# A two-layer hybrid trunk on one core: stationary-weight products as three matmuls of 256 columns in one PSUM bank instead of 512 and 256 in two

## The chip, the cores and the metric

The kernel runs on one core of one Trainium2 chip, with one launch. The metric is the device time of the program in microseconds. TensorE (PE in the profile, with its weight loads under PEld) multiplies, VectorE (DVE) and ScalarE (ACT) work element by element, GpSimd (POOL) does little here, and SyncE (SP) issues nearly all transfers.

## The reference

256 tokens of width 2048 in float32 go through two layers. Cut to what matters:

```python
for layer in range(2):
    if layer == 0:
        x = x + hybrid_mixer(rms_norm(x, hyb_norm), w_in, ..., w_out)   # SSD heads and stick-breaking attention
    else:
        x = x + multiscale_pool(rms_norm(x, pool_norm), pool_w, pool_b, pool_scale)
    u = relu(rms_norm(x, mlp_norm[layer]) @ w_up[layer])                # 2048 -> 8192
    x = x + (u * u) @ w_down[layer]                                     # 8192 -> 2048
```

`hybrid_mixer` projects with `w_in` (2048 columns wide input, about 11,300 columns of output: z, x, B, C, dt, q, k, v), runs a causal convolution, a chunked state-space scan and an attention with stick-breaking weights, and projects with `w_out`.

## The kernel before, in words

**The weight stream.** All products with weights form one list of units (`plan`, lines 47 to 90). A unit is a block of output columns; a step of it is the part of its weights that one DMA brings. The main loop (lines 789 to 827) goes through units and steps in this order; `feed` loads steps ahead (line 161, six ahead) and splits them ahead (lines 182 and 183, three ahead).

**Three products for one.** Each float32 weight is split into a high part (ScalarE, line 182, tile `hi`) and the rest (VectorE, line 183, tile `lo`), and so are the activations: a token tile is `[128, 2, 4, 256]`, that is high and low, four k-tiles, 256 tokens, and the high and low parts of one k-tile stand 4 x 256 float32 = 4 KB apart in a partition. A product is then high x high, high x low and low x high, accumulated in PSUM.

**Two kinds of units.** In most units the tokens are stationary: line 820 loads 128 tokens of a k-tile as weights and streams up to 512 columns of `hi` or `lo`; for each of the two halves of the tokens (m = 0, 1) there are three such matmuls into one bank. The last 512 columns of the last "down" product are cut into two units of 256 columns. In the units marked `turned` the weights are stationary, so that the result has the channels on the partitions: the unit c1, the eight units x of the input projection and the 64 units "up" of the two MLPs, 73 in all, each with 16 k-tiles and 256 output columns in two halves f of 128. Here line 812 loads the 128 columns of `hi` and streams 512 columns, the high part and the low part of the tokens side by side, into one bank for f; and line 814 loads the 128 columns of `lo` and streams the 256 columns of the high part into the first half of the same bank. Each f has a bank of its own. At the end the two halves of each bank must be added.

**The end of a unit.** `finish` reads the accumulators. For turned units `add_halves` (lines 269 to 272) copies the second halves of both banks to SBUF on ScalarE (line 271) and adds the first halves on VectorE (line 272). Then `turned` (line 325) multiplies by the norm's scale per token, and for "up" units line 746 takes the maximum with 0 and multiplies by the same scale.

**Order of the work.** Each engine does its instructions in the order in which the program issues them. Work that is not a product with weights (norms, transposes, convolution, scan, attention) is written as generators in two queues, `lane` and `lane2`; after each step of the stream `tick` advances them by a piece, so their small matmuls stand between those of the stream. The accumulators are two tiles of two banks (`ps_main`, line 791), used in turn, so a unit can begin while the one before is read out.

Of the kernel before, what the change touches and what calls it, by code (L numbers as in the profile page):

```python
# [13 lines left out]
ALU = mybir.AluOpType  # L14
# [3 lines left out]
T = 256  # L18
# [6 lines left out]
NB = DFF // FB  # L25
WINS = (2, 4, 8, 16)

# columns of the input projection: z | x | B | C | dt | q | k | v
CZ, CX, CB, CC = 0, 2048, 4096, 4608
CQ, CK, CV = 5152, 7200, 9248  # L30

# per-partition parameters (channel = tile * 128 + partition)
P_HYB, P_MLP, P_POOL, P_CW, P_CB, P_ON, P_QN, P_KN = 0, 16, 48, 64, 160, 184, 200, 201
NPRM = 202

# constant matrices
K_ID, K_U, K_SL, K_ONE, K_LT = 0, 128, 256, 384, 512
NCST = 640

# where in the weight stream (unit, k-tile) the quarters of x for the first norm are loaded  # L40
X_EARLY = ((0, 14), (1, 2), (1, 6), (1, 10))
AHEAD_LOAD = 6
WARM = 2
# [1 line left out]


def plan():
    """The products with weights in their order. A unit is a block of output columns; a step is
    the part of its weights that one DMA brings: [128, k-tiles, columns]."""
    units = []  # L50

    def unit(w, r0, nk, c0, n, kind, arg, src, k0=0, turned=False):
        units.append(dict(w=w, r0=r0, nk=nk, c0=c0, n=n, kind=kind, arg=arg, src=src, k0=k0,
                          turned=turned))

    unit("w_in", 0, KT, CB, 512, "b", None, "h")
    unit("w_in", 0, KT, CC + 256, 288, "c2", None, "h")
    unit("w_in", 0, KT, CC, 256, "c1", None, "h", turned=True)
    for g in range(4):
        for h in range(2):  # L60
            unit("w_in", 0, KT, CX + 512 * g + 256 * h, 256, "x", (g, h), "h", turned=True)
        unit("w_in", 0, KT, CZ + 512 * g, 512, "z", g, "h")
    for j in range(4):
        unit("w_in", 0, KT, CK + 512 * j, 512, "k", j, "h")
        unit("w_in", 0, KT, CQ + 512 * j, 512, "q", j, "h")
        unit("w_in", 0, KT, CV + 512 * j, 512, "v", j, "h")
    for c in range(4):
        unit("w_out", 0, 2 * KT, 512 * c, 512, "out", c, "merged")
    for layer in range(2):
        if layer == 1:  # L70
            for g in range(4):
                unit("pool_w", 512 * g, 4, 0, 512, "pool", g, "pool", 4 * g)
        for b in range(NB):
            for i in range(8):
                unit("w_up", D * layer, KT, b * FB + 256 * i, 256, "up", (layer, b, i),
                     f"mlp{layer}", turned=True)
            for c in range(4):
                n = 256 if (layer, b, c) == (1, NB - 1, 3) else 512
                for c0 in range(512 * c, 512 * c + 512, n):
                    unit("w_down", DFF * layer + b * FB, KT, c0, n, "down", (layer, b, c), "u")  # L80

    steps, off = [], 0
    for u, d in enumerate(units):
        ks = list(range(0, d["nk"], 4 if d["turned"] else 2))
        if u == 0:
            ks = [0, 1, 2, 3] + ks[2:]
        for k, e in zip(ks, ks[1:] + [d["nk"]]):
            steps.append((u, k, e - k, off))
            off += (e - k) * P * d["n"]
    return units, steps  # L90
# [3 lines left out]
def tile_trunk(ctx: ExitStack, tc: tile.TileContext, x_in, xt_in, w_all, prm_in,  # L94
# [27 lines left out]
    def v3(ap, a, b):  # L122
        return ap.rearrange("p (a b) -> p a b", a=a, b=b)

    # ------------------------------------------------------------ constants
    x_sb = []
    cst = new("cst", [P, NCST])
    prm = new("prm", [P, NPRM])
# [7 lines left out]
        return prm[:, i : i + 1]  # L136

    def load_x(q):
        """half of the tokens' rows, half of the columns at a time"""
        m, c = q // 2, slice(D // 2 * (q % 2), D // 2 * (q % 2) + D // 2)  # L140
        if q == 0:
            x_sb[:] = [slot(12 + m, (P, D), F32) for m in range(MT)]
        nc.sync.dma_start(x_sb[m][:, c], x_in[m * P : m * P + P, c])

    # ------------------------------------------------------------ the weight stream
    hT, merged = {}, {}
    u_blk, pT, hM = {}, {}, [{}, {}]
    sources = {"h": hT, "merged": merged, "pool": pT, "mlp0": hM[0], "mlp1": hM[1], "u": u_blk}
# [42 lines left out]
            split(done["split"])  # L191
            done["split"] += 1

    # ------------------------------------------------------------ work beside the weight stream
    lane, lane2 = deque(), deque()
    flags = set()

# [14 lines left out]
            assert lane or lane2  # L212
            tick()

    # ------------------------------------------------------------ norms
    def power(dst, src, mean):
        """dst = (src * mean + eps) ** -0.5"""
        n = src.shape[-1]
        t = new("pw", [P, 8], bufs=2)[:, :n]
        dve.tensor_scalar(t, src, mean, EPS, ALU.mult, ALU.add)  # L220
        pool.tensor_tensor(dst, t, mhalf[:, :n], ALU.pow)  # L221

    def put_hi_lo(dst, c, ps, gain=None):
        """dst[:, 0/1, c] = the high and low parts of ps (times a per-partition gain)"""
        if gain is None:
            act.activation(dst[:, 0, c], ps, AF.Copy)  # L226
            dve.tensor_tensor(dst[:, 1, c], ps, dst[:, 0, c].bitcast(F32), ALU.subtract)  # L227
        else:
            act.activation(dst[:, 0, c], ps, AF.Copy, scale=gain)  # L229
            dve.scalar_tensor_tensor(dst[:, 1, c], ps, gain, dst[:, 0, c].bitcast(F32),  # L230
                                     ALU.mult, ALU.subtract)

    def to_ring(src, tiles, kt0, dst, gain):
        """src[m]: [128 tokens, 512]; four k-tiles of 256 tokens into dst and tiles[kt0...]"""
        for h in range(2):
            b = bank()
            bv = v3(b, 2, T)
# [15 lines left out]
    rs = {}  # L253

    def spread(name):
        """rs[name, "row"][p, t] = rs[name] of token t, for all p"""
        r = rs[name]
        dg = v3(t4(2 * P), MT, P)
        for m in range(MT):
            dve.tensor_scalar(dg[:, m], ident, r[:, m : m + 1], None, ALU.mult)  # L260
        yield
        b = bank()
        for m in range(MT):
            pe.matmul(b[:, m * P : (m + 1) * P], ones, dg[:, m], start=True, stop=True)
        o = new("rrow", [P, T], bufs=2)
        dve.tensor_copy(o, b[:, :T])
        rs[name, "row"] = o

    def add_halves(dst, ps):
        """dst = the sum of the two halves of each bank"""  # L270
        act.activation(dst, ps[:, :, T:], AF.Copy)  # L271
        dve.tensor_tensor(dst, ps[:, :, :T], dst, ALU.add)  # L272

    def row2(name):
        return rs[name, "row"][:, None, :].to_broadcast([P, 2, T])
# [19 lines left out]
        if c == 3 and name != "pool":  # L295
            yield from spread(name)

    # ------------------------------------------------------------ SSD
    ssd = {}

    def evac(ps, n, r):
# [3 lines left out]
        return e  # L305

    def turn(e, n):
        """e: [tokens, n * 128 channels] -> [channel, n, 3 + 256 tokens]"""
        yield
        yield  # L310
        xT = v3(t4(n * 259), n, 259)
# [9 lines left out]

    def turned(ps):
        xT = v3(t4(2 * 259), 2, 259)
        add_halves(xT[:, :, 3:], ps)
        dve.tensor_tensor(xT[:, :, 3:], xT[:, :, 3:], row2("hyb"), ALU.mult)
        return xT

    def conv(xT, ct0, n, dst):
        """xT: [channel, n, 3 + 256 tokens] -> dst [channel, n, 256 tokens] = silu(conv + b)"""
        dve.memset(xT[:, :, 0:3], 0.0)  # L330
        for c in range(n):
            w = P_CW + 4 * (ct0 + c)
# [7 lines left out]
                yield  # L340

    def gen_dt(pre):
        """pre: [128, 64] dt before softplus, (chunk, head)"""
        e, t, q, da = (ssd["tmp"][:, 1792 + 64 * i : 1856 + 64 * i] for i in range(4))
        # log1p(e) = 2 artanh(e / (2 + e)), e = exp(-|pre|) in (0, 1]
        act.activation(e, pre, AF.Abs)
        act.activation(e, e, AF.Exp, scale=-1.0)
        dve.tensor_scalar(t, e, 2.0, None, ALU.add)
# [153 lines left out]
        dst = slot(8 + g)  # L502
        yield from to_ring(lambda m: y[:, m], merged, 4 * g, dst, P_ON)

    # ------------------------------------------------------------ stick-breaking attention
    at = {}

    def gen_qk(kind, j, e):
# [113 lines left out]
                merged[16 + 4 * j + 2 * i + h] = (dst, 2 * i + h)  # L622
            yield

    # ------------------------------------------------------------ MLP and pooling
    def gen_u(i, ea, eb, base):
        yield
        act.activation(eb, ea, AF.Square)  # L628
# [36 lines left out]
    def finish(u, ps):  # L665
# [73 lines left out]
        elif kind == "up":  # L739
# [2 lines left out]
            need(lambda: (name, "row") in rs)  # L742
            e = ev()
            ea, eb = v3(e[:, 0], 2, T), v3(e[:, 1], 2, T)
            add_halves(ea, ps)
            dve.scalar_tensor_tensor(ea, ea, 0.0, row2(name), ALU.max, ALU.mult)  # L746
            lane.append(gen_u(i, ea, eb, ((4, 8), (0, 4))[layer][b % 2]))

    # ------------------------------------------------------------ the stream
    act.dma_start(prm, prm_in)  # L750
    act.preload_act_table_set("silu_and_others")
    mhalf = new("mhalf", [P, 8])
    pool.memset(mhalf, -0.5)
    # keeps the tensor engine's clock up until the first weights are there
    wt = new("ev", [P, MT, 512], bufs=3)
    dve.memset(wt[:, 0], 0.0)
    wb = bank()
# [3 lines left out]
    hx, late = [], []  # L761

    def startup():
        """the first norm's scale and small constants"""
        ss = new("ss", [P, MT, 4], bufs=2)
        for q in range(4):
            m, h = q // 2, q % 2
# [21 lines left out]
    for u, d in enumerate(units):  # L789
# [5 lines left out]
        while i < len(steps) and steps[i][0] == u:  # L795
# [10 lines left out]
            for kk in range(n2):  # L806
                t, c = src[k0 + k + kk]
                first, last = k + kk == 0, k + kk == nk - 1
                if d["turned"]:
                    for f in range(2):  # L810
                        fs = slice(f * P, f * P + P)
                        pe.matmul(ps[:, f].rearrange("p (h t) -> p h t", h=2), hi[:, kk, fs],  # L812
                                  t[:, :, c], start=first, stop=False)
                        pe.matmul(ps[:, f, :T], lo[:, kk, fs], t[:, 0, c], start=False, stop=last)  # L814
                    continue
                parts = [(m, h) for m in range(MT) for h in range(3)]
                if u == 0:
# [74 lines left out]
```

## Time and profile before

| what | value |
|---|---|
| median of three runs | 2215.83 us (2215.49 to 2216.3) |
| span of the profiled execution | 2214.3 us |
| granted TensorE clock | 1.000 |
| TensorE busy, instructions | 2207.0 us, 11045 (and as many weight loads) |
| VectorE busy | 1325.4 us |
| ScalarE busy | 1113.0 us |
| GpSimd busy | 21.7 us |
| read from HBM | 412.57 MB, 187 GB/s |

The profile is of one execution; what lies around its span is not in it, and the median of the runs is 1.5 us above the span. A row of a group gives line, engine, operation, output and inputs, shape, count, then busy time in us and mean duration of one in ns, then the engine's idle time just before these instructions and who ended it. Matmuls are pipelined: the next begins while the one before still drains, so their durations add up to more than the time they take.

### The profile page before, as it was taken

How to read it: one execution, taken by the hardware profiler on the slowest of the kernel's cores; microseconds unless marked ns; L12 is line 12 of the kernel's file. 1: busy time of each engine (PE TensorE's matmuls, PEld its weight loads, DVE VectorE, ACT ScalarE, POOL GpSimd, SP SyncE). 2: the span in 40 equal slices, each digit the busy share in tenths (PEclk: the TensorE clock that was granted, in tenths of full speed). 3: DMA queues.
4: the chain of work that ended last, by engine and by line, in shares of the span. 5: the costliest groups of instructions: out<-in, count | busy, mean ns of one | idle time of the engine just before them, and what ended most of it. 6: DMA issues, size and time to landing. Idle time of an engine off the chain costs nothing.

```text
span 2214.3 us, 28392 instructions
## 1 busy us (share of the span) xinstructions
PE 2207.0 (100%) x11045; PEld 1854.0 (84%) x11045; DVE 1325.4 (60%) x1554; ACT 1113.0 (50%) x1325; POOL 21.7 (1%) x21
## 2 busy tenths in 40 slices
PE   9999999999999999999999999999999999999999
PEld 7888888888888888888888888888888888888888
DVE  6988756655645565555555466577555645655654
ACT  7665456665544454354344345456534534544543
POOL 0000000000000000000000000000000000000000
PEclk9999999999999999999999999999999999999999
DMA  8654555555665566556566666555666656565564
GB/s 300 213 196 162 163 184 167 163 179 170 202 187 184 181 186 186 189 186 189 187 189 190 204 219 190 181 171 163 190 196 187 188 189 190 187 193 191 190 195 148
DMA packets 118630, 416.56 MB, mean 188 GB/s; under 512 B 13344, under 2 KB 16096, under 8 KB 118240
## 3 DMA queue, kind: packets, MB, share of 16 engines
q1 hardware_dynamic: 117632, 413.60, 59.0%
q8 instruction: 86, 1.41, 0.3%
q10 hardware_dynamic: 864, 1.15, 0.2%
q14 instruction: 48, 0.39, 0.1%
HBM read 412.57 MB, written 2.13 MB: 187 GB/s over the span
## 4 chain that ended last, share of the span: by engine, by line
PE 99%; DMA 0%; DVE 0%; ACT 0%; issue 0%; SPq 0%; DVEq 0%; ACTq 0%
PE acc L820 58%; PE acc L812 25%; PE acc L814 13%; PE bg L469 1%; PE bg L241 1%; DMA raw<-w_all 0%; PE bg L526 0%; PE bg L616 0%; PE bg L561 0%; PE bg L437 0%; PE bg L557 0%; PE bg L618 0%; PE bg L474 0%; PE bg L480 0%; DVE lo L183 0%; PE bg L577 0%
## 5 line engine op out<-in xcount | busy, mean ns | idle before, releaser
L183 DVE TENSOR_TENSOR lo<-raw,hi 128x1024 fp32r<-128x1024 f32 (+2 forms) x774 | 931.4, 1205 | 777.5 <-ACT hi L182 762.9
L182 ACT ACTIVATE hi<-raw 128x1024 fp32r<-128x1024 f32 (+2 forms) x774 | 808.5, 1045 | 1033.8 <-PE acc L820 642.7
L820 PE MATMUL acc<-hi,st 128*128 128x512 f32 (+2 forms) x3840 | 1175.2, 389 | 1.4 <-ACT hi L182 1.4
L820 PEld LDWEIGHTS acc<-hi,st 128*128 128x128 f32 x3840 | 709.9, 188 | 153.4 <-ACT hi L182 3.5
L812 PE MATMUL acc<-st,hi 128*128 128x512 f32 x2336 | 826.1, 398 | 0.0
L820 PE MATMUL acc<-lo,st 128*128 128x512 f32 (+2 forms) x1920 | 740.7, 387 | 0.1
L814 PE MATMUL acc<-st,lo 128*128 128x256 f32 x2336 | 654.8, 280 | 0.0
L812 PEld LDWEIGHTS acc<-st,hi 128*128 128x128 f32 x2336 | 438.3, 188 | 106.1 <-issue 1.4
L814 PEld LDWEIGHTS acc<-st,lo 128*128 128x128 f32 x2336 | 440.5, 189 | 2.0 <-issue 1.2
L820 PEld LDWEIGHTS acc<-lo,st 128*128 128x128 f32 x1920 | 360.4, 188 | 78.1 <-DVE lo L183 0.5
L706 DVE TENSOR_TENSOR st<-st,acc 128x512 f32<-128x512 f32 (+1 forms) x74 | 46.5, 669 | 29.1 <-PE acc L820 29.1
L746 DVE SCALAR_TENSOR_TENSOR ev<-ev,rrow 128x512 f32<-128x512 f32 x64 | 44.3, 692 | 2.2
L227 DVE TENSOR_TENSOR st<-ev,st 128x512 fp32r<-128x512 f32 x64 | 44.3, 692 | 0.2
L272 DVE TENSOR_TENSOR ev<-acc,ev 128x512 f32<-128x512 f32 x64 | 43.7, 683 | 0.0
L226 ACT ACTIVATE st<-ev 128x512 fp32r<-128x512 f32 x64 | 40.6, 634 | 2.0
L229 ACT ACTIVATE st<-bg,prm 128x256 fp32r<-128x256 f32 x64 | 28.4, 468 | 24.9 <-DVE st L230 22.8
L628 ACT ACTIVATE ev<-ev 128x512 f32<-128x512 f32 x64 | 39.5, 617 | 0.0
L271 ACT ACTIVATE ev<-acc 128x512 f32<-128x512 f32 x64 | 37.2, 582 | 0.0
L230 DVE SCALAR_TENSOR_TENSOR st<-bg,prm,st 128x256 fp32r<-128x256 f32 x64 | 29.4, 478 | 6.0 <-ACT st L229 6.0
L336 DVE SCALAR_TENSOR_TENSOR t<-t,prm,t 128x256 f32<-128x256 f32 x48 | 19.6, 476 | 0.0
L221 POOL TENSOR_TENSOR qrs<-pw,mhalf 128x8 f32<-128x8 f32 x8 | 15.6, 1952 | 246.4 <-DVE pw L220 246.4
L516 DVE TENSOR_TENSOR ev<-ev,qrs 128x1024 f32<-128x1024 f32 x8 | 9.8, 1225 | 13.5 <-POOL qrs L221 13.5
(155 smaller groups left out, 595.7 us busy)
## 6 DMA issues: line engine op xcount, KB each, us to landing
raw<-w_all SPq DMA_DIRECT2D x746, 512.0 KB, 3.5
raw<-w_all SPq DMA_DIRECT2D x20, 256.0 KB, 3.1
st<-x_in SPq DMA_DIRECT2D x8, 512.0 KB, 5.3
st<-scr SPq DMA_DIRECT2D x8, 512.0 KB, 5.8
raw<-w_all SPq DMA_DIRECT2D x8, 288.0 KB, 4.5
st<-prow_in SPq DMA_DIRECT2D x2, 1024.0 KB, 5.3
st<-xt_in SPq DMA_DIRECT2D x6, 256.0 KB, 6.3
st<-pmat_in SPq DMA_DIRECT2D x1, 768.0 KB, 5.1
```

What stands on the lines that cost most here:

```text
L182: act.activation(hi, raw, AF.Copy)
L183: dve.tensor_tensor(lo, raw, hi.bitcast(F32), ALU.subtract)
L226: act.activation(dst[:, 0, c], ps, AF.Copy)
L227: dve.tensor_tensor(dst[:, 1, c], ps, dst[:, 0, c].bitcast(F32), ALU.subtract)
L271: act.activation(dst, ps[:, :, T:], AF.Copy)
L272: dve.tensor_tensor(dst, ps[:, :, :T], dst, ALU.add)
L628: act.activation(eb, ea, AF.Square)
L706: dve.tensor_tensor(x_sb[m][:, cs], x_sb[m][:, cs], ps[:, m, : d["n"]], ALU.add)
L746: dve.scalar_tensor_tensor(ea, ea, 0.0, row2(name), ALU.max, ALU.mult)
L812: pe.matmul(ps[:, f].rearrange("p (h t) -> p h t", h=2), hi[:, kk, fs], t[:, :, c], start=first, stop=False)
L814: pe.matmul(ps[:, f, :T], lo[:, kk, fs], t[:, 0, c], start=False, stop=last)
L820: pe.matmul(ps[:, m, :n], t[:, h % 2, c, m * P : (m + 1) * P], (hi, hi, lo)[h][:, kk], start=first and h == 0, stop=last and h == 2)
```

## The change

For turned units, the matmul of 512 columns is replaced by two of 256, both into the same columns of PSUM, and the matmul with `lo` goes there too; both halves f share one bank, the first in columns 0 to 255, the second in 256 to 511. So there are three matmuls of 256 columns for each half and k-tile, each with its own weight load (the first two load the same `hi` columns). Only the very first matmul of a unit has the start flag. `add_halves` is gone: the finishing VectorE instruction reads the bank. The rest of the diff removes comments and docstrings.

```diff
-    def add_halves(dst, ps):
-        """dst = the sum of the two halves of each bank"""
-        act.activation(dst, ps[:, :, T:], AF.Copy)
-        dve.tensor_tensor(dst, ps[:, :, :T], dst, ALU.add)
...
     def turned(ps):
         xT = v3(t4(2 * 259), 2, 259)
-        add_halves(xT[:, :, 3:], ps)
-        dve.tensor_tensor(xT[:, :, 3:], xT[:, :, 3:], row2("hyb"), ALU.mult)
+        dve.tensor_tensor(xT[:, :, 3:], v3(ps[:, 0], 2, T), row2("hyb"), ALU.mult)
         return xT
...
             ea, eb = v3(e[:, 0], 2, T), v3(e[:, 1], 2, T)
-            add_halves(ea, ps)
-            dve.scalar_tensor_tensor(ea, ea, 0.0, row2(name), ALU.max, ALU.mult)
+            dve.scalar_tensor_tensor(ea, v3(ps[:, 0], 2, T), 0.0, row2(name), ALU.max, ALU.mult)
...
                 if d["turned"]:
                     for f in range(2):
                         fs = slice(f * P, f * P + P)
-                        pe.matmul(ps[:, f].rearrange("p (h t) -> p h t", h=2), hi[:, kk, fs],
-                                  t[:, :, c], start=first, stop=False)
-                        pe.matmul(ps[:, f, :T], lo[:, kk, fs], t[:, 0, c], start=False, stop=last)
+                        for h in range(3):
+
+                            pe.matmul(ps[:, 0, f * T : f * T + T], (hi, hi, lo)[h][:, kk, fs],
+                                      t[:, h % 2, c], start=first and h == 0 and f == 0,
+                                      stop=last and h == 2, skip_group_check=True)
                     continue
```

## The prediction

> **What bounds the kernel now.** I began with the page: span, busy engines, and the chain of work that ended last.
>
> ```profile
> span 2214.3 us, 28392 instructions
> PE 2207.0 (100%) x11045; PEld 1854.0 (84%) x11045; DVE 1325.4 (60%) x1554; ACT 1113.0 (50%) x1325; POOL 21.7 (1%) x21
> ...
> q8 instruction: 86, 1.41, 0.3%
> ...
> PE 99%; DMA 0%; DVE 0%; ACT 0%; issue 0%; SPq 0%; DVEq 0%; ACTq 0%
> ...
> L820 PE MATMUL acc<-hi,st 128*128 128x512 f32 (+2 forms) x3840 | 1175.2, 389 | 1.4 <-ACT hi L182 1.4
> ...
> L812 PE MATMUL acc<-st,hi 128*128 128x512 f32 x2336 | 826.1, 398 | 0.0
> ...
> L814 PE MATMUL acc<-st,lo 128*128 128x256 f32 x2336 | 654.8, 280 | 0.0
> L812 PEld LDWEIGHTS acc<-st,hi 128*128 128x128 f32 x2336 | 438.3, 188 | 106.1 <-issue 1.4
> ...
> L746 DVE SCALAR_TENSOR_TENSOR ev<-ev,rrow 128x512 f32<-128x512 f32 x64 | 44.3, 692 | 2.2
> ...
> L272 DVE TENSOR_TENSOR ev<-acc,ev 128x512 f32<-128x512 f32 x64 | 43.7, 683 | 0.0
> ...
> L271 ACT ACTIVATE ev<-acc 128x512 f32<-128x512 f32 x64 | 37.2, 582 | 0.0
> ```
>
> TensorE holds 99% of the chain, and its lines show hardly any idle time before them (1.4, 0.0 and 0.0 us). VectorE and ScalarE are busy 60% and 50% of the time and hold 0% of the chain. So the end is set by the rate at which TensorE takes matmuls, one after another, and by nothing else over any length. The mean durations (398 and 280 ns) are of no use as prices, because matmuls overlap. What counts is the distance from one start to the next. For that I read the chain in order of time, whose long pieces are unbroken runs of one line, and then the timeline of TensorE. In the chain, columns are start, length, line and count:
>
> ```profile
> by line: PE acc L820 58.2%; PE acc L812 24.6%; PE acc L814 12.5%; PE bg L469 0.6%; PE bg L241 0.6%; DMA raw<-w_all 0.4%; PE bg L526 0.3%; PE bg L616 0.3%; PE bg L561 0.3%; PE bg L437 0.2%; PE bg L557 0.2%; PE bg L618 0.2%; PE bg L474 0.2%;
> ...
> 834.33 89.57 PE acc L820 x384
> 1014.35 88.53 PE acc L820 x384
> ...
> 1588.09 87.08 PE acc L820 x384
> 1764.81 89.58 PE acc L820 x384
> 1944.03 87.08 PE acc L820 x384
> 2120.75 89.76 PE acc L820 x480
> ```
>
> Between two runs of L820 lies one block of eight "up" units with stationary weights: 8 units x 16 k-tiles x 2 column halves = 256 pairs of one matmul of 512 columns (L812) and one of 256 (L814). In layer 0 such a block lasts from 834.33 + 89.57 = 923.90 to 1014.35, which is 90.45 us or 353.3 ns a pair. In layer 1 it lasts from 1588.09 + 87.08 = 1675.17 to 1764.81, 89.64 us or 350.2 ns a pair; the next lies between 1854.39 and 1944.03, again 89.64. These are the prices of before, all small stalls included.
>
> **The price of three times 256.** The kernel already contains a stretch of the new kind: its last 512 columns of output are done as two units of 256 columns (192 matmuls of L820, each with its own weight load, three in a row into the same columns of one bank). The timeline of TensorE, at the start and at the end of that stretch:
>
> ```profile
> 2187.77 0.40 PE L820 MATMUL acc<-hi,st 128*128 128x256 f32 x2
> 2188.01 0.29 PE L820 MATMUL acc<-lo,st 128*128 128x256 f32 x1
> 2188.13 0.40 PE L820 MATMUL acc<-hi,st 128*128 128x256 f32 x2
> 2188.37 0.28 PE L820 MATMUL acc<-lo,st 128*128 128x256 f32 x1
> 2188.49 0.39 PE L820 MATMUL acc<-hi,st 128*128 128x256 f32 x2
> ...
> 2210.22 0.27 PE L820 MATMUL acc<-lo,st 128*128 128x256 f32 x1
> ```
>
> From the first start to the start of the 192nd are 2210.22 - 2187.77 = 22.45 us over 191 steps: 117.5 ns each, so 352.6 ns for three. That is the same as the 350.2 and 353.3 ns of the pairs. In the pairs themselves the single 256 (L814) shows the same step, here in a layer-1 block:
>
> ```profile
> 1690.65 0.28 PE L814 MATMUL acc<-st,lo 128*128 128x256 f32 x1
> 1690.77 0.39 PE L812 MATMUL acc<-st,hi 128*128 128x512 f32 x1
> 1691.00 0.28 PE L814 MATMUL acc<-st,lo 128*128 128x256 f32 x1
> 1691.11 0.39 PE L812 MATMUL acc<-st,hi 128*128 128x512 f32 x1
> 1691.34 0.28 PE L814 MATMUL acc<-st,lo 128*128 128x256 f32 x1
> ```
>
> L814 to L812 is 0.12, 0.11 us; L812 to L814 is 0.23. So one 512 costs about two 256s, though the second 256 brings a weight load with it.
>
> **The sum for TensorE.** The change replaces 2336 pairs (73 units x 32) by 2336 triples; 2336 matmuls and as many weight loads are added, and the columns streamed stay 768. At 352.6 ns a block of 256 triples takes 90.27 us. The four blocks of layer 0 gain 4 x 0.18 = 0.7 us. The four of layer 1 lose 4 x 0.63 = 2.5 us. That leaves the 288 pairs of the input projection (c1 and x): the chain gives L812 and L814 together 37.1% of 2214.3 = 821.5 us, less 4 x 90.45 + 4 x 89.64 = 720.4, so 101.1 us or about 351 ns each (the first block of layer 0 taken as the others; rounded shares allow 7 ns either way). They lose 288 x 1.6 ns = 0.5 us. Sum: +2.3 us.
>
> That step of 117.5 ns is the number on which all hangs: 1 ns of it is 3 x 2336 ns = 7.0 us. It differs from the new code in its operands: there the tokens are loaded and the weights stream, here it is the other way round. Its neighbours bound it. For the low end: the fastest runs of 512 (87.08 us / 384 = 226.8 ns) give 113.4 halved. For the high end: a triple in the stretch above took 0.36 us once or twice, 120 a step. I take the middle, because the 192 steps are the only ones with 256 after 256, and the pairs' own 256 agrees.
>
> **The sum for the other engines.** Per turned unit one ScalarE pass (L271, 582 ns) and one VectorE pass (L272, 683 ns) go: 73 x 0.582 = 42 us and 73 x 0.683 = 50 us of busy time. What remains (L746, 692 ns, now reading PSUM) costs about the 683 ns of L272, which reads PSUM too. On the path this is worth nothing: the chain gives both engines 0%, and a unit's bank is wanted again only a unit later (11.2 us) while its readers take under 2 us. What TensorE waits for on ScalarE in the whole kernel is one row of the waits, and the groups of the first 30 us, before the first turned unit, hold all of it:
>
> ```profile
> PEld acc L820 <- ACT hi L182: 3.5, 4, 1.3
> ...
> L820 PEld LDWEIGHTS acc<-hi,st 128*128 128x128 f32 x70 | 12.9, 189 | 5.8 <-ACT hi L182 3.5
> ```
>
> So a less busy ScalarE takes away no wait; if it needed the time, 42 us are now free. A bank that only VectorE reads may also save a wait ahead of a unit: the weight-load queue of L812 has such instructions.
>
> ```profile
> L812 PEldq EVENT_SEMAPHORE  x6: 51/51/51, 1873.5 to 1929.5; - x6
> ```
>
> At 51 ns for 64 units that is 3.3 us at most; L812's idle time is 0.0, so they lie under running matmuls and I take 0. Instruction fetch grows with the added matmuls and loads: 1.41 MB for 22,090 of them becomes 1.71 MB, still 0.3 to 0.4% of the transfer engines' time. No DMA is moved or added, and no engine gets a new wait.
>
> **A rule against the change.** Weight loads last 188 ns (L812 PEld) and fill 84% of the span; 2336 more of them, laid end to end, would make 1854.0 + 439.2 = 2293 us. In the stretch of 256s the view by windows shows what such loads do:
>
> ```profile
> 2191.00:2213.00 22.00, 19.49 (x167) 19.29 (x165) 9.03 (x15) 6.71 (x11) 0.00 (x0) 1.00 0.43 131
> ```
>
> Columns: window, length, TensorE, weight loads, VectorE, ScalarE, POOL, clock. Loads are busy 19.29 of 19.49 us, 165 of them, or 117 ns each though one lasts 188. So they overlap one another, and full occupancy did not slow the steps. The Trainium skill (Perfetto Trace Analysis, Identifying the Most-Contended Engine) tells one to judge TensorE's headroom by the busy share of LDWEIGHTS, not of matmuls. By that rule the added loads eat all that is left and 79 us more; by the trace they cost nothing up to this step.
>
> **The rivals.**
> *A fixed cost for each added matmul* (slower). The last block of L820 runs 288 matmuls of 512 from 2120.75 to 2187.77, 232.7 ns each, and then the 256s, two of which take 235.1: 2.4 ns for splitting one. If the pairs keep their 256 and split their 512 at that price everywhere, 2336 x 2.4 = +5.6 us, 2221.4. For it: one clean comparison on the same tokens. Against: layer 0 pays 353.3 for a pair, more than 352.6. The Trainium skill (TensorE: Matmul & The Clock Gate, "Wait — 56ns, not 53.3ns?") has such a term, about 2.5 ns a matmul. By it the time would be 2215.8 + 5.8 = 2221.6; the trace agrees, with its 2.4 ns.
>
> *The weight load becomes the limit* (slower). In the pairs every second load hides under a 512; in the triples none does. If loading freshly written weights takes 120 ns a step rather than 117.5, the point from which it decides, a triple costs 360: 2336 x 8.3 ns (against a mean of 351.7) = +19 us, 2235. For it: loads are at 99% in the stretch above, with no room. Against: the load for each L812 already has only the 256 of the L814 before it to hide under.
>
> *The 512 of two pieces was slow* (faster). L812 streams two pieces 4 KB apart and pays 233 ns (24.6% of the span over 2336) where some runs of L820 pay 226.8. If pieces of one stretch run at half the fast pace plus half the splitting price, 113.4 + 1.2 = 114.6, a triple costs 343.8: 2336 x 7.9 = -18 us, 2197. For it: two speeds of 512 exist. Against: the pairs' single 256, already in one piece, shows 0.11 to 0.12.
>
> *Waits go with the evacuation*: the 3.3 us above, 2215.8 + 2.3 - 3.3 = 2214.8. Against: L812's idle time of 0.0.
>
> **How the numbers follow.** The median of the runs, 2215.83, is 1.5 us above the span; the sum is a difference and goes on the median: 2215.8 + 2.3 = 2218.1. Within 0.2% means 2211.4 to 2220.3, about what a measurement of this kernel can tell from no change. My case (0.46), with 1 ns either way on the step, reaches from 2211 to 2225: 0.29 same, 0.13 slower, 0.04 faster. Fixed cost (0.14): 0.09 slower, 0.05 same. Weight load (0.15): slower. Faster pieces (0.20): 0.19 faster, 0.01 same. Waits (0.05): same. Together 0.23 faster, 0.40 same, 0.37 slower. The range, 2203 to 2235, leaves out the far half of the weight-load case and most of the faster pieces, under 0.2.
>
> **What to look for.** TensorE with 13,381 matmuls and as many loads, VectorE and ScalarE with 73 instructions fewer each and some 50 and 42 us less busy. In the chain in order of time, a block between two runs of the 512s near 90.3 us in both layers: then my step is right; layer 0 a little shorter than before, layer 1 longer. Blocks of 92 us would speak for the weight load, 88 us for the faster pieces; unchanged blocks with a shorter span for the waits. Matmuls of 256 in a repeated pattern of unequal steps would say that operands' places matter more than their size, and that my price from other operands was the wrong one.

## The result, and the profile after

The changed kernel takes 2235.89 us (four runs, 2234.88 to 2236.59) against 2215.97 for the kernel before: a ratio of 1.0092, with a 95% interval of 1.0079 to 1.0106. It is 19.9 us slower. The forecast was 2218.1 with a range of 2203 to 2235.

From the page of the changed kernel, where line 807 is the new matmul and 815 the one with stationary tokens (line 820 before):

```profile
span 2233.1 us, 33041 instructions
PE 2226.7 (100%) x13381; PEld 1980.0 (89%) x13381; DVE 1281.6 (57%) x1481; ACT 1071.2 (48%) x1248; POOL 21.5 (1%) x21
...
q8 instruction: 104, 1.70, 0.3%
...
PE 99%; DVE 0%; ACT 0%; DMA 0%; SPq 0%; issue 0%; DVEq 0%
...
L807 PE MATMUL acc<-st,hi 128*128 128x256 f32 x4672 | 846.6, 284 | 0.1
...
L807 PEld LDWEIGHTS acc<-st,hi 128*128 128x128 f32 x4672 | 727.7, 191 | 4.6 <-issue 2.9
...
L739 DVE SCALAR_TENSOR_TENSOR ev<-acc,rrow 128x512 f32<-128x512 f32 x64 | 44.3, 692 | 44.7 <-PE acc L807 44.7
```

The counts are as the text of the change says: 2336 more matmuls and loads, VectorE 44 us and ScalarE 42 us less busy (the forecast had 50 and 42; on VectorE the passes left took some more in all). TensorE still holds 99% of the chain and hardly waits (0.1 us before L807), and L739, which now reads PSUM, waits for TensorE and not TensorE for it. So nothing new holds TensorE up; it takes longer for its own work. The chain in order of time (start, length, line, count) shows where, now with both kinds of runs unbroken:

```profile
754.26 83.78 PE acc L807 x696
838.04 89.56 PE acc L815 x384
927.60 92.14 PE acc L807 x768
...
1108.27 92.14 PE acc L807 x768
...
1599.59 87.06 PE acc L815 x384
1686.64 92.11 PE acc L807 x768
1778.75 89.56 PE acc L815 x384
1868.31 92.10 PE acc L807 x768
```

The down blocks (L815) are as they were, 89.56 and 87.06 us. An up block of 768 matmuls takes 92.14 us in layer 0 and 92.11 in layer 1, that is 120.0 ns a step in both, where before it took 90.45 and 89.64. Three such blocks of layer 0 lose 1.7 us each, three of layer 1 lose 2.5 each, the first block of each layer (with other work between) 1.4 and some 2.7, and the input projection and attention before them 2.3 (the first long run begins at 754.26; in the trace of before at 751.93). Together that is about 19 us, the whole difference of the spans (2233.1 - 2214.3 = 18.8).

The timeline of TensorE inside a block shows steps of 0.36 us for a triple, where the forecast had 0.353:

```profile
1110.13 0.28 PE L807 MATMUL acc<-st,lo 128*128 128x256 f32 x1
1110.26 0.40 PE L807 MATMUL acc<-st,hi 128*128 128x256 f32 x2
1110.49 0.28 PE L807 MATMUL acc<-st,lo 128*128 128x256 f32 x1
1110.62 0.40 PE L807 MATMUL acc<-st,hi 128*128 128x256 f32 x2
```

### The profile page after: what moved, and what is told of

It is laid out like the page before. It is cut to its first block, busy times and chain, and to the rows that moved or that the text cites. A ratio compares the mean times of both kernels' runs of the same rounds, so it can differ in the third digit from the quotient of the medians.

```text
span 2233.1 us, 33041 instructions
## 1 busy us (share of the span) xinstructions
PE 2226.7 (100%) x13381; PEld 1980.0 (89%) x13381; DVE 1281.6 (57%) x1481; ACT 1071.2 (48%) x1248; POOL 21.5 (1%) x21
## 4 chain that ended last, share of the span: by engine, by line
PE 99%; DVE 0%; ACT 0%; DMA 0%; SPq 0%; issue 0%; DVEq 0%
PE acc L815 58%; PE acc L807 38%; PE bg L463 1%; PE bg L241 1%; PE bg L520 0%; PE bg L610 0%; PE bg L555 0%; DMA raw<-w_all 0%; PE bg L551 0%; PE bg L612 0%; PE bg L431 0%; PE bg L474 0%; PE bg L468 0%; PE bg L571 0%; PE bg L570 0%
## 5 line engine op out<-in xcount | busy, mean ns | idle before, releaser
L815 PE MATMUL acc<-hi,st 128*128 128x512 f32 (+2 forms) x3840 | 1175.0, 389 | 0.6 <-ACT hi L182 0.6
L807 PE MATMUL acc<-st,hi 128*128 128x256 f32 x4672 | 846.6, 284 | 0.1
L815 PEld LDWEIGHTS acc<-hi,st 128*128 128x128 f32 x3840 | 710.2, 188 | 151.9 <-ACT hi L182 2.5
L815 PE MATMUL acc<-lo,st 128*128 128x512 f32 (+2 forms) x1920 | 740.8, 387 | 0.1
L807 PEld LDWEIGHTS acc<-st,hi 128*128 128x128 f32 x4672 | 727.7, 191 | 4.6 <-issue 2.9
L807 PE MATMUL acc<-st,lo 128*128 128x256 f32 x2336 | 660.7, 283 | 0.0
L807 PEld LDWEIGHTS acc<-st,lo 128*128 128x128 f32 x2336 | 445.9, 191 | 0.0
L815 PEld LDWEIGHTS acc<-lo,st 128*128 128x128 f32 x1920 | 360.3, 188 | 78.1 <-DVE lo L183 0.7
L739 DVE SCALAR_TENSOR_TENSOR ev<-acc,rrow 128x512 f32<-128x512 f32 x64 | 44.3, 692 | 44.7 <-PE acc L807 44.7
L449 DVE TENSOR_SCALAR st<-st,acs 128x128 f32<-128x128 f32 x64 | 13.9, 284 | 5.6 <-DMA st<-scr 5.6
L278 ACT ACTIVATE t<-st 128x512 f32<-128x512 f32 x24 | 15.1, 628 | 2.5 <-DVE st L655 2.2
```

The lines of the kernel that those rows point to most:

```text
L739: dve.scalar_tensor_tensor(ea, v3(ps[:, 0], 2, T), 0.0, row2(name), ALU.max, ALU.mult)
L807: pe.matmul(ps[:, 0, f * T : f * T + T], (hi, hi, lo)[h][:, kk, fs], t[:, h % 2, c], start=first and h == 0 and f == 0, stop=last and h == ...
L815: pe.matmul(ps[:, m, :n], t[:, h % 2, c, m * P : (m + 1) * P], (hi, hi, lo)[h][:, kk], start=first and h == 0, stop=last and h == 2)
```

## The experiments

The question was why a 256 costs 120.0 ns here and 117.5 in the last stretch of the kernel before. Theory at first: the added load with its matmul costs that much, whatever surrounds it. Rivals: adding three times into one bank; loading the same columns twice running; the load as a floor under the step; the place of the operands.

**Only the split.** The kernel before with its 512 as two 256s into the two halves of the bank; banks, halves and their addition as before.

```diff
-                        pe.matmul(ps[:, f].rearrange("p (h t) -> p h t", h=2), hi[:, kk, fs],
-                                  t[:, :, c], start=first, stop=False)
+                        for h in range(2):
+                            pe.matmul(ps[:, f, h * T : h * T + T], hi[:, kk, fs], t[:, h, c],
+                                      start=first and h == 0, stop=False, skip_group_check=True)
...
```

> Only the 512 is split into two matmuls of 256, each with its weight load; the banks, the halves and their addition stay as before. If the added weight load with its matmul is what costs (theory: every load and matmul of this form takes 120 ns), a block of eight up units takes 92.0 us as in the changed kernel and the time is about 2236 us. If adding three times into the same columns, or both halves in one bank, is what costs (rival), the blocks stay at 90.4 and 89.6 us and the time near 2217 us.

Measured: 2235.38 us, 1.0093 of before (1.0076 to 1.011). The chain in order of time of this kernel:

```profile
838.49 89.56 PE acc L822 x384
1020.20 88.53 PE acc L822 x384
```

Between the two runs lie 1020.20 - 928.05 = 92.15 us, the changed kernel's block. So the split alone makes the whole loss, the accumulation in one bank costs nothing, and the dropped ScalarE and VectorE passes, which this kernel still has, are worth nothing that shows: 2235.38 with them, 2235.89 without.

**Another order.** The changed kernel with the `lo` matmul between the two of `hi`.

```diff
-                            pe.matmul(ps[:, 0, f * T : f * T + T], (hi, hi, lo)[h][:, kk, fs],
-                                      t[:, h % 2, c], start=first and h == 0 and f == 0,
+                            pe.matmul(ps[:, 0, f * T : f * T + T], (hi, lo, hi)[h][:, kk, fs],
+                                      t[:, h // 2, c], start=first and h == 0 and f == 0,
```

> The changed kernel with the three matmuls in the order hi x high, lo x high, hi x low, so that no two neighbouring loads read the same columns, except across the end of a triple where they differ as well. If a load costs the same whatever it reads (theory), steps stay at 120 ns and a block at 92.0 us, about 2236 us. If loading the same columns twice running is what costs (rival), only the repeated load is slow and the block falls towards 90.3 us, about 2219 us.

Measured: 2238.2 us, a single run. The up blocks take 92.14 and 92.11 us, to 0.01 us those of the changed kernel; the rest is in the first 620 us. Loading the same columns twice running is not the cause.

**Shorter streams.** The changed kernel with fewer tokens streamed in the inner k-tiles of the up units; it leaves out part of the products.

```diff
+SCAN = ((64, 128, 160, 192), (208, 224, 240, 248))
...
+                    m_n = T
+                    if d["kind"] == "up" and not first and not last:
+                        m_n = SCAN[d["arg"][0]][d["arg"][1]]
...
-                            pe.matmul(ps[:, 0, f * T : f * T + T], (hi, hi, lo)[h][:, kk, fs],
-                                      t[:, h % 2, c], start=first and h == 0 and f == 0,
+                            pe.matmul(ps[:, 0, f * T : f * T + m_n], (hi, hi, lo)[h][:, kk, fs],
+                                      t[:, h % 2, c, :m_n], start=first and h == 0 and f == 0,
```

> The changed kernel with shorter streams: in the up units all k-tiles but the first and the last stream only the first 64, 128, 160, 192 tokens (the four blocks of layer 0) and 208, 224, 240, 248 tokens (layer 1) instead of 256, so part of the products is left out. If the weight load is the floor under a step of 120 ns, the step stays near 120 ns at 248, 240, 224 and below. If a step is its columns plus a fixed cost of 13 ns, it falls by 0.417 ns a column: 117 at 248, 113 at 240, 107 at 224, until a floor.

Measured: 2256.68 us, a single run. It is longer than the changed kernel because of the block with 64 columns, which took 129.91 us (see the last section). The chain in order of time shows the blocks with 128, 160, 192, 224, 240 and 248 columns:

```profile
980.85 86.53 PE acc L810 x768
...
1155.91 86.58 PE acc L810 x768
...
1332.08 86.48 PE acc L810 x768
...
1722.62 86.45 PE acc L810 x768
...
1898.65 86.62 PE acc L810 x768
...
2072.34 89.02 PE acc L810 x768
```

Of the 768 steps of a block 96 still stream 256 columns; at 120.0 ns they take 11.52 us. The other 672 take (86.53 - 11.52) / 672 = 111.6 ns at 128 columns, 111.5 at 224, 111.8 at 240 and 115.3 at 248. So there is a floor under a load with its matmul, about 111.6 ns, but 256 columns lie above it: from 248 to 256 the step still grows by 4.7 ns. The load as the limit, the rival that had named 120 ns a step and 2235 us, falls as a mechanism. A step is its columns and something more: with 226.7 ns for a 512 in the fast down blocks and 120.0 for a 256 it is 0.417 ns a column and 13.3 ns besides. That is a line through two points: it gives 113.3 and 116.6 ns at 240 and 248 columns, and 111.8 and 115.3 were measured.

**Down units in 256s.** The kernel before with every 512 of the down units in two, the up units as they were.

```diff
+                cut = 256 if d["kind"] == "down" else n
                 for m, h in parts:
-                    pe.matmul(ps[:, m, :n], t[:, h % 2, c, m * P : (m + 1) * P],
-                              (hi, hi, lo)[h][:, kk], start=first and h == 0, stop=last and h == 2)
+                    for q in range(0, n, cut):
+                        pe.matmul(ps[:, m, q : q + cut], t[:, h % 2, c, m * P : (m + 1) * P],
+                                  (hi, hi, lo)[h][:, kk, q : q + cut],
+                                  start=first and h == 0 and q == 0, stop=last and h == 2,
+                                  skip_group_check=True)
```

> The kernel before with every matmul of 512 columns of the down units cut into two of 256, each with its own weight load of the same tokens; the up units are untouched. Before, blocks of 384 took 87.1 us with tokens in some slots and 89.6 us in others. If a step is its columns plus 13 ns, a block of 768 takes 92.2 us whatever the slots. If the place of the stationary tokens decides (117.5 ns in the last stretch of before), the blocks in the slots of the 89.6 us take 90.2 us and the others less, about 88.5 us. In both cases the up blocks stay at 90.4 and 89.6 us.

Measured: 2231.08 us, a single run. The chain in order of time, one row for each down block:

```profile
833.07 90.23 PE acc L822 x768
1012.06 91.12 PE acc L822 x768
1193.62 90.24 PE acc L822 x768
1591.87 92.15 PE acc L822 x768
1773.67 90.24 PE acc L822 x768
1953.47 92.15 PE acc L822 x768
```

Here one and the same line has both prices: 92.15 / 768 = 120.0 ns where the tokens lie in slots 0 to 3 (the fourth and sixth rows), 90.24 / 768 = 117.5 where they lie in slots 4 to 7, and half of each in slots 8 to 11. The blocks that were fast with 512s (87.08 us) are the slow ones with 256s, and the other way round. So splitting a 512 costs 240.0 - 226.7 = 13.3 ns in some slots and 235.0 - 233.3 = 1.7 in others. One line with one shape has two prices here, and they go with the slots, as the second theory of this run had it; but the slots that it did not name got dearer (92.15 us) where it had them cheaper (88.5).

**Which places?** In the compiled program hi, lo, raw and the slots 0 to 3, 8 and 9 begin 96 bytes past a multiple of 256 in their partition (and alike modulo 4096); slots 4 and 7 begin 128 past one, 5 and 6 64, 10 and 11 192. So, modulo 256 bytes, 4 and 7 start 32 bytes past hi and lo, 5 and 6 32 short of them, 10 and 11 96 past them. The profiles show no places; these differences also follow from the order in which the code first asks for its tiles, and their sizes. Four runs try it. The first leaves all starts and lays the parts of a token tile side by side:

```diff
-    def slot(i, shape=(P, 2, 4, T), dt=F32R):
+    def slot(i, shape=None, dt=F32R):
+        if shape is None:
+            return new(f"st{i}", [P, 4, 2, T], dt).rearrange("p c h t -> p h c t")
         return new(f"st{i}", list(shape), dt)
```

> The kernel before with the token tiles laid out so that the high and low parts of a k-tile stand side by side in a partition (nothing else changes): the 512 of a pair is one piece of 512 columns instead of two of 256 lying 4 KB apart. If the two pieces make the 512 dear, a pair falls to 226.7 + 120.0 = 346.7 ns, a block to 88.8 us, the time to about 2205 us. If a matmul costs its columns plus a share that hangs on where the operands stand (theory), the piecing alone changes the blocks by less than 0.3 us and the time stays near 2215 us.

Measured: 2214.61 us, 0.9998 of before (0.9989 to 1.0008), and all whole blocks as before to 0.01 us. That the 512 comes in two pieces costs nothing; the "512 of two pieces was slow" of the rivals falls.

The next two move all tiles behind `mhalf` by 32 bytes, in the kernel before and in the changed one.

```diff
-    mhalf = new("mhalf", [P, 8])
+    mhalf = new("mhalf", [P, 16])
```

> The kernel before with one small tile 32 bytes longer, which moves every later tile by 32 bytes in its partition: hi, lo, and the token slots 0 to 3, 8 and 9 now begin on multiples of 64 bytes, and slots 4 to 7, 10 and 11, which did before, now 32 bytes beside them. If the place of the loaded operand decides the step of a 512 (theory), the two speeds of the down blocks change sides: 87.1 us becomes 89.6 and the other way round, and the pairs, whose loaded operand is hi and lo, change too. If only the place of loaded and streamed operand to each other counts (rival), the down blocks stay as they were. If places play no part, nothing changes anywhere. Time by the theory between 2200 and 2220 us.

> The changed kernel with the same shift by 32 bytes. By the theory the loaded hi and lo then stand as the tokens of slots 4 to 7 did in the last stretch of before, and the 256s cost 117.5 instead of 120.0 ns: blocks of 90.2 us, time near 2218 us, less or more by what the down blocks win or lose. If the added weight load is dear for another reason (rival), the blocks stay at 92.1 us and the time near 2236 us.

Measured: 2215.66 us, 1.0005 of before (0.9996 to 1.0015), and 2236.11 us, 1.0095 (1.008 to 1.011). Every block is as it was. So where an operand stands by itself does not count, at least for a move by 32 bytes; what is left is places relative to each other, or no part of places at all. The next run, on the kernel before, has this shift and 32 bytes more ahead of slot 4, which changes the distance of slots 4 to 7, 10 and 11 from hi and lo.

```diff
+            new("pad", [P, 8])
             ssd["bc"] = slot(4, (P, 8, T), F32)
```

> The kernel before with the shift and a further unused 32 bytes ahead of slot 4, so that hi, lo and all token slots begin on multiples of 64 bytes. If the place of the loaded operand alone decides, all down blocks take 89.6 us and the pairs as in the run with the shift alone. If the place of the two operands to each other counts, all down blocks take 87.1 us, some 10 us less in all. If being on multiples of 64 bytes helps both reads, all blocks are shorter than any before, under 87 us.

Measured: 2210.46 us, 0.998 of before (0.9971 to 0.9989). The chain in order of time:

```profile
833.25 88.42 PE acc L821 x384
1012.13 88.21 PE acc L821 x384
...
1584.61 87.07 PE acc L821 x384
1761.80 88.41 PE acc L821 x384
```

The blocks of slots 4 to 7 fall from 89.57 to 88.42, nearly the mean of fast and slow. In this program slots 5 and 6 begin at the same place modulo 256 bytes as hi and lo, slots 4 and 7 do not. Inside one block the timeline of TensorE shows it where the tokens pass from slot 6 to slot 7, at 849.60 (the 72 matmuls of slots 4 to 6 lie before it):

```profile
848.24 0.62 PE L821 MATMUL acc<-hi,st 128*128 128x512 f32 x2
...
848.92 0.62 PE L821 MATMUL acc<-hi,st 128*128 128x512 f32 x2
...
849.60 0.63 PE L821 MATMUL acc<-hi,st 128*128 128x512 f32 x2
...
850.30 0.63 PE L821 MATMUL acc<-hi,st 128*128 128x512 f32 x2
...
851.00 0.63 PE L821 MATMUL acc<-hi,st 128*128 128x512 f32 x2
```

Three matmuls take 0.68 us before that point (226.7 ns each) and 0.70 after it (233.3). Over the whole block, from start to start, a 512 took 226.6 to 227.9 ns in slots 5 and 6 and 233.2 to 233.3 in slots 4 and 7. Being on a multiple of 64 bytes is not what helps; the distance between loaded and streamed operand is.

**All at one place, and none.** All slots, hi, lo and raw are reserved first, so that their starts agree modulo 4096; this in the kernel before and in the changed one. Then, in the changed one, raw, hi and lo are moved by 96 bytes against all slots (the line marked with !). A move by 1312 bytes, the distance of slot 4 in the kernel before, needed more room than a partition has, so there is no time for it.

```diff
+    for i in range(14):
+        slot(i)
!    new("pad", [P, 24])
+    for tag, n in (("raw", 4), ("hi", 4), ("lo", 4)):
+        new(tag, [P, 1024], F32 if tag == "raw" else F32R, bufs=n)
```

> The kernel before with all token slots and the weight tiles reserved first, one behind the other, so that every slot, hi and lo begin at the same place modulo 4096 bytes. Theory: where the loaded and the streamed operand stand at the same place modulo some 256 bytes, a step is its columns plus 13.3 ns (512: 226.7, 256: 120.0); elsewhere a 512 costs 230 to 233 and a 256 117.5. Then all down blocks take 87.1 us, the last stretch of 256s 120.0 ns a step, and some 2300 slow steps of 512 save 6.6 ns each: 2214.5 - 15 = about 2200 us. If places play no part, all stays as before, 2214.5 us.

> The changed kernel with the tiles reserved in the same way. Theory: the triples stay at 360.0 ns, blocks at 92.1 us, and the down blocks gain what they gain in the kernel before with the same places: about 2221 us, as far above that kernel as the change alone stands above before, or a little more. If the triples were dear because of the places of some slots (rival), their blocks fall below 92 us.

> The changed kernel with the token slots reserved first and raw, hi and lo behind them moved by 96 bytes, so that loaded and streamed operand never stand at the same place modulo 256 bytes. If place decides the step of a 256 also with weights loaded (as it does with tokens loaded), the triples fall to 352.6 ns and their blocks to 90.3 us. If with loaded weights a step is 120.0 ns on average wherever the tokens stand, the blocks stay at 92.1 us. In both cases the down blocks are slow throughout, 88.4 to 89.6 us.

Measured: 2201.94 us, 0.994 of before (0.9926 to 0.9953); 2220.24 us, 1.0023 (1.0014 to 1.0033); 2237.45 us in a single run. The chain of the kernel before with all at one place:

```profile
828.65 87.05 PE acc L823 x384
1006.14 87.06 PE acc L823 x384
...
1573.85 87.08 PE acc L823 x384
1751.37 87.06 PE acc L823 x384
```

The chain of the changed kernel with all at one place (L819 for the down blocks, L811 for the triples):

```profile
833.73 87.07 PE acc L819 x384
920.79 92.15 PE acc L811 x768
```

The chain of the changed kernel with hi and lo moved (here L820 stands for the down blocks and L812 for the triples):

```profile
845.22 89.59 PE acc L820 x384
934.81 90.11 PE acc L812 x768
...
1602.32 89.59 PE acc L820 x384
1691.91 90.11 PE acc L812 x768
```

With equal places every down block is fast, and the kernel before takes 13.2 us less; the triples of the changed kernel stay dear and its disadvantage remains (2220.24 against 2201.94). With hi and lo moved, every down block is slow, and the triples cost 90.11 / 256 = 352.0 ns instead of 360. So the forecast's price was right for operands at this distance and wrong for those of the changed kernel. The cheaper triples did not make the kernel faster, 2237.45 us against 2235.89: the down blocks, up to 2.5 us longer, and the stretch before the first long run of triples, 8.1 us longer (762.36 against 754.26), took the gain back. The kernel before was not run with hi and lo moved, so what the split costs at this distance is not known.

**Grouped.** The kernel before with equal places and the four matmuls of a k-tile in another order, first both 512s and then both 256s.

```diff
                     for f in range(2):
                         fs = slice(f * P, f * P + P)
                         pe.matmul(ps[:, f].rearrange("p (h t) -> p h t", h=2), hi[:, kk, fs],
                                   t[:, :, c], start=first, stop=False)
+                    for f in range(2):
+                        fs = slice(f * P, f * P + P)
                         pe.matmul(ps[:, f, :T], lo[:, kk, fs], t[:, 0, c], start=False, stop=last)
```

> The kernel before with all places the same, and the four matmuls of a k-tile reordered: the two 512s (hi, both column halves) first, then the two 256s (lo), instead of 512, 256, 512, 256. If each matmul costs its columns plus 13.3 ns whatever its neighbours, four of them take 693.3 ns instead of the measured 706.7, a block 88.75 us instead of 90.44, and the time falls by 8 x 1.7 and a little more to about 2188 us. If the changing size of the stream is not what makes a pair 6.7 ns dearer than that, blocks stay at 90.4 us and the time at about 2202 us.

Measured: 2192.97 us, 0.9902 of before (0.9886 to 0.9919). This version beats both kernels, by 21.6 us and by about 43. Its chain:

```profile
828.50 87.05 PE acc L825 x384
1004.72 87.05 PE acc L825 x384
```

An up block takes 1004.72 - 915.55 = 89.17 us instead of 90.44, so the order saves 1.3 us a block, somewhat less than the 1.7 expected. That the changing size is what cost them is not shown. In the timeline of this run a 512 right ahead of another 512 still takes 233 ns from start to start, and in the run with the down units in 256s one block of untouched pairs, with the sizes in turn, took 1012.06 - 923.30 = 88.76 us, less than the grouped ones.

## Why the prediction was wrong, point by point

**What bounds the kernel**: right. TensorE's own rate sets the end before and after; evacuation and its waits moved the time by nothing, as the run with the split alone shows with both passes still in.

**The price of before** (353.3 and 350.2 ns a pair): right, it was read in the blocks themselves.

**The price of three 256s**: this step failed. The forecast took 117.5 ns from the last 192 matmuls, noted that they differ in their operands, and let that stand as 1 ns of uncertainty: "I take the middle, because the 192 steps are the only ones with 256 after 256, and the pairs' own 256 agrees." Those matmuls read tokens in slots 4 to 7, which stand elsewhere modulo 256 bytes than hi and lo. The triples read tokens in slots 0 to 3 in layer 0 and 8 to 11 in layer 1. With equal places a 256 costs 120.0. The missed 2.5 ns, three times in each of 2336 triples, are 17.5 us, and 2218.1 + 17.5 = 2235.6. The sign was in the rows quoted: two speeds of 512s, 226.8 and 233.3, in blocks that differ by their slots alone. It was used for the low end and for one rival; that a place that is fast for a 512 is the dear one for a 256 was not thought of. So layer 0, which was to gain 0.7 us, lost some 6.5, and layer 1 lost some 10 where 2.5 were forecast. Of the signs that the forecast named, blocks of 92 us came and pointed to the weight load, which was not the cause. Unequal steps of 256s, its sign for the operands' places, came in slots 10 and 11 of layer 1 alone; in layer 0, where all places are equal, the steps are an even 120 ns.

**"The pairs' own 256 agrees"**: it does not carry over. After a 512 the 256 took 117 ns, among 256s at equal places 120.0. In the pairs of layer 0 the extra time sits in the 512 (353.3 - 117 = 236 in place of 226.7).

**The rivals.** The fixed cost of an added matmul was right in kind and mis-sized: 2.4 ns from the last stretch, 13.3 with equal places. Of that, 6.6 ns in layer 0 and 3.5 in layer 1 are made up for by pairs that cost more than 226.7 + 120.0 = 346.7; the rest, 6.7 and 9.8, is the loss. The Trainium skill (TensorE: Matmul & The Clock Gate, "Wait — 56ns, not 53.3ns?") has about 2.5 ns; the down blocks in 256s come near it at unequal places (1.7) and not at equal ones (13.3), and the measurement decides. The weight-load rival had the right number, 2235, by luck: the shorter streams refute its reason. The Trainium skill's rule on the busy share of weight loads (Perfetto Trace Analysis, Identifying the Most-Contended Engine) was reckoned in the forecast at 79 us more; the loads filled 89% of the span (1980.0 us, not 2293), since neighbouring ones overlap.

**The chances.** 0.37 stood on slower, but the range ended at 2235, which left out the far half of the case that came.

**What stays open.** Why equal places give one price and unequal ones another was not found; only distances were tried. In layer 1 of the changed kernel the slots 10 and 11 stand at another place than hi and lo, and the triples there still averaged 120.0 ns, with uneven steps of 115 to 127, while the move by 96 bytes the other way gave 117.3. So not every unequal distance is cheap, and the places account for the 120.0 ns of layer 0 and of half of layer 1, but not of the other half. Pairs too have several prices at the same places: in the run with down units in 256s one untouched up block took 88.76 us instead of 90.44.

## What to carry to other kernels

A price taken from the same instruction with the same shapes holds only as far as its operands stand in the same way to each other; where a trace shows two speeds of one shape, find out which one the new code will get before multiplying it by thousands. On a kernel bound by the rate of its matmuls, count instructions as well as columns: at equal places and in unbroken runs of one size each cost 13.3 ns beyond its columns, so two matmuls of 256 were dearer than one of 512, and passes saved on engines off the path paid for none of it. Reserving the large tiles first, so that they start alike, and issuing the two 512s of a k-tile before its two 256s were worth 1% here.

## What the runs showed of the hardware that was not expected

Where tiles start relative to each other changes a matmul's step: 226.7 or 233.3 ns for 512 columns, 120.0 or 117.5 for 256, and the order of the two turns round. A load with its matmul had a floor of about 111.6 ns, reached at 240 columns. In the block with streams of 64 columns the granted clock was lower, here in the view by windows (last columns: clock, share of the transfer engines, GB/s):

```profile
800.00:880.00 80.00, 80.00 (x436) 80.00 (x434) 28.31 (x29) 25.08 (x29) 0.00 (x0) 0.59 0.36 119
985.00:1060.00 75.00, 75.00 (x668) 75.00 (x667) 43.25 (x42) 37.46 (x42) 0.00 (x0) 1.00 0.62 197
```

The first row is the block with 64 columns: clock 0.59 and 436 matmuls in 80 us, 183 ns each. The second is that with 128: full clock and 112 ns. Half the columns took longer, though the view has TensorE busy all the time in both. This is one run, and why the clock fell is not shown.
